# Two transformer blocks on one core: first norm over four tiles, weights' second parts on VectorE, late tiles of the final norm by halves

## The chip, the core and the metric

The kernel runs on one core of a Trainium2 chip. The metric is the time of one execution on the device, in microseconds (us). TensorE multiplies, VectorE (DVE), ScalarE (ACT) and GpSimd (POOL) work element by element, and SyncE (SP) issues most transfers; ACT and POOL issue some. Each engine works off its own queue in order.

## The reference

Two blocks follow one another on x, 1024 tokens of 1024 channels in f32. The parts that the change touches:

```
y = rmsnorm(h, norm_mix_g) @ w_in            # first block: 1024 x 2560
q, k, v = ...; a, g = the last 2 x 512 columns of y
att  = dilated_sliding_attention(q, k, v)    # after a partial rotary of q and k
conv = silu(layernorm(depthwise_conv31(a * sigmoid(g))))
h = h + concat(att, conv) @ w_out
... cross attention, MLP, the whole second block ...
out = rmsnorm(h, lnf_g_2)                    # the final norm
```

## The kernel before

**Precision.** Every f32 operand of a product is cut into a rounded first part (hi, ScalarE, line 128 or 131) and a second part, the rest (lo = src - hi, lines 129 and 132); three matmuls give one product. Weights are split in halves of 512 rows by `w_s` (line 139): a 512 KB load into one of two `raw` buffers, hi on ScalarE, lo on `b.wlo`. A `raw` buffer takes the next load when both parts have been read. The parts lie in 12 `w` tiles, four to a set of weights, which are used in turn.

**Start** (`mix_part`). Eight tiles of 128 tokens are loaded, with the first weights between them. `norm_T` takes them in pairs: sum of squares on ScalarE (line 267), a chain of small VectorE instructions for the inverse root (`rsqrt`, line 244), a scaling (line 293), then 16 TensorE transposes (line 240) whose 128x256 results are split into `xT` (lines 131, 132). `xT[0]` holds tokens 0 to 511, `xT[1]` the rest; a product with `xT[0]` needs tiles 0 to 3.

**First projections.** For each half of the a and g columns, `gemm_s` (line 206) makes g and a for two groups of 128 channels, first over `xT[0]`, then over `xT[1]`: 16 products of 24 matmuls. ScalarE takes tanh of g (line 443), VectorE forms u (line 448). Then v: 16 tiles of 24 matmuls (lines 177 to 179), each copied out of PSUM by ScalarE (line 470) into one of four `t2k` buffers and stored by SP (line 471). Then q and k: four sets of weights, eight half passes of four tiles each, with the rotary on VectorE (line 493) and a transposed, split copy to memory (`stage`).

**Convolution.** Its 120 taps (line 422, one VectorE instruction each, 128 x about 1016) lie in a background list; `pump(us)` takes from the list at set points, at a booked cost of 1.1 for a tap.

**Order.** The instructions of each engine are put in a fixed order when the program is built, by a scheduler with its own model of durations: of what its model calls ready it takes what was written earliest; `high_priority(offset=400)` counts as written 400 instructions earlier, and `issue_after(ins)` keeps what follows behind `ins` on the same engine.

**End.** In the last MLP product `ff_down` makes the last three of the 112 steps tile by tile, so the sums for half 0 of tiles 4, 5, 6 and 7 come one after another. `final_norm` (line 1222) goes through the tiles in order: `finish` adds the late sum (line 1068), ScalarE squares both halves (line 1231), VectorE finds the inverse root for the one tile, scales both halves with the gain (line 1240), and SP and ScalarE store them (line 1243). The next tile's add is issued behind the scaling of the tile before.

Of the kernel before, what the change touches and what calls it, by code (L numbers as in the profile page):

```python
# [12 lines left out]
BF16 = mybir.dt.bfloat16  # L13
AF = mybir.ActivationFunctionType
ALU = mybir.AluOpType
# [4 lines left out]
P = 128  # L20
S = 1024
D = 1024
KT = D // P
NT = S // P
EPS = 1e-6
# [4 lines left out]
def fp(ap):  # L30
    return ap.bitcast(F32)


class Builder:
# [90 lines left out]
    def split(self, hi, lo, src, scale=None, eng=None):  # L125
        nc = self.nc
        if scale is None:
            nc.scalar.activation(hi, src, AF.Copy)  # L128
            (eng or nc.vector).tensor_tensor(out=lo, in0=src, in1=fp(hi), op=ALU.subtract)  # L129
        else:  # L130
            nc.scalar.activation(hi, src, AF.Copy, scale=scale)
            nc.vector.scalar_tensor_tensor(
                out=lo, in0=src, scalar=scale, in1=fp(hi), op0=ALU.mult, op1=ALU.subtract
            )

    def wtile(self, shape, dt=F32R, name="w"):
        return self.wpool.tile(list(shape), dt, tag="w", name=self.nm(name))

    def w_s(self, *parts):


        tiles = []
        for hf in range(2):
            raw = self.rpool.tile([P, 4, 256], F32, tag="raw", name=self.nm("raw"))
            c = 0
            for w in parts:
                n = w.shape[1]
                self.wq.dma_start(
                    out=raw[:, :, c : c + n],
                    in_=w[hf * 512 : (hf + 1) * 512, :].rearrange("(k p) n -> p k n", p=P),  # L150
                )
                c += n
            hi, lo = self.wtile([P, 4, 256]), self.wtile([P, 4, 256])
            self.split(hi, lo, raw, eng=self.wlo)
            tiles.append((hi, lo))

        def get(k, c0, c1):
            hi, lo = tiles[k // 4]
            return hi[:, k % 4, c0:c1], lo[:, k % 4, c0:c1]

        return get

    def w_t(self, w):

# [191 lines left out]
def mem_norm(b):  # L356
    nc = b.nc
    raw = []
    for t in range(2):
        r = b.slot(29 + t, name="mem")  # L360
        nc.sync.dma_start(out=r, in_=b.i["mem"][0, t * P : (t + 1) * P, :])
        raw.append(r)
    tl = [b.slot(20 + n, (P, 4, 256), F32R, "memT") for n in range(4)]
    memT = [(tl[k // 4][:, k % 4, :], tl[2 + k // 4][:, k % 4, :]) for k in range(KT)]
    b.norm_T(raw, b.g_mem, [memT], 2)
    return memT
# [22 lines left out]
def mix_part(b):  # L389
    nc, i = b.nc, b.i  # L390
    w_in = i["w_in"][0]
    b.xk_d = b.dram.tile([4, P, 2, 2, 256], F32, name="xk_d")
    b.xv_d = b.dram.tile([4, P, 2, 2, 256], F32, name="xv_d")
    b.wlo = nc.gpsimd
    xc = i["x"][0].rearrange("(l c) d -> c l d", c=4)
    raw = [b.slot(16 + t, name="x") for t in range(NT)]
    load = lambda t: nc.sync.dma_start(out=raw[t], in_=xc[t // 2, (t % 2) * P : (t % 2 + 1) * P, :])
    (g_mix,) = b.columns("g_mix", [i["norm_mix_g"].rearrange("a (k p) -> (a k) p", p=P)], nc.scalar)
    for t in range(4):
        load(t)  # L400
    wg0 = b.w_s(w_in[:, 2048:2304])
    for t in range(4, NT):
        load(t)
    wa0 = b.w_s(w_in[:, 1536:1792])
    xT = b.halves(range(0, 8), range(8, 16))
    b.norm_T(raw, g_mix, xT, 2)
    b.consts()


# [22 lines left out]
    for half in range(2):  # L432
        wg = b.w_s(w_in[:, 2304:2560]) if half else wg0
        wa = b.w_s(w_in[:, 1792:2048]) if half else wa0
        for js in ((0,), (1,)):
            for mm in range(2):
                m = 2 * half + mm
                if js == (0,):
                    th[m] = b.slot(24 + mm, name="th")
                    u[m] = b.slot(26 + m, name="u")  # L440

                def ev_g(j, ps, m=m):
                    nc.scalar.activation(th[m][:, j * 512 : j * 512 + 512], ps, AF.Tanh, scale=0.5)

                def ev_a(j, ps, m=m):
                    o = u[m].rearrange("p (l c) -> p c l", c=4)[:, 2 * j : 2 * j + 2, :]
                    v3 = lambda a: a.rearrange("p (c l) -> p c l", c=2)
                    nc.vector.scalar_tensor_tensor(
                        out=o, in0=v3(th[m][:, j * 512 : j * 512 + 512]), scalar=1.0, in1=v3(ps),
                        op0=ALU.add, op1=ALU.mult,  # L450
                    )

                b.gemm_s(wg, mm * P, xT, ev_g, js)
                b.gemm_s(wa, mm * P, xT, ev_a, js)
                if js == (1,):
                    conv_ops(m)
                    if m:
                        b.pump(7)
        if half == 0:
            memT = mem_norm(b)  # L460

# [2 lines left out]
    for n in range(2):  # L464
        w = b.w_s(w_in[:, 1024 + n * 256 : 1024 + n * 256 + 256])
        for t in range(NT):
            ps = b.mm()
            b.mm3(ps[:, :256], [(x, w(k, 0, 256)) for k, x in enumerate(b.tok(xT, t))])
            st = b.t2k((P, 256))
            nc.scalar.copy(out=st, in_=ps[:, :256])  # L470
            nc.sync.dma_start(out=b.v_d[t * P : (t + 1) * P, n * 256 : n * 256 + 256], in_=st)
            b.pump(3.5)


# [3 lines left out]
    for p in range(4):  # L478
        w = b.w_s(w_in[:, p * P : p * P + P], w_in[:, 512 + p * P : 512 + p * P + P])
        for half in range(2):  # L480
            y = b.slot((24, 25, 30)[(2 * p + half) % 3], (P, 4, 256), name="y")
            for t4 in range(4):
                ps = b.mm()
# [9 lines left out]
            tt = lambda o, a, c, op: nc.vector.tensor_tensor(out=o, in0=a, in1=c, op=op)  # L493
# [58 lines left out]
    last = []  # L552
# [21 lines left out]
    h = [b.slot(16 + t, name="h") for t in range(NT)]  # L574
# [636 lines left out]
def finish(b, t, after):  # L1211

    if t in b.late:
        with b.tc.high_priority(offset=400), b.tc.issue_after(after.ins):
            b.late.pop(t)()
# [5 lines left out]

def final_norm(b, h, g, out):

    nc = b.nc
    last = None
    for t in range(NT):
        finish(b, t, last)
        sq = b.small(2, "fsq")
        for n in range(2):
            junk = b.slot(8 + (2 * t + n) % 8, (P, 512), BF16, "junk")  # L1230
            nc.scalar.activation(junk, h[t][:, n * 512 : n * 512 + 512], AF.Square, accum_out=sq[:, n : n + 1])
        ms = b.small(1, "fms")
        nc.vector.tensor_scalar(
            out=ms, in0=sq[:, 0:1], scalar1=sq[:, 1:2], scalar2=1.0 / D, op0=ALU.add, op1=ALU.mult
        )
        nc.vector.tensor_scalar(out=ms, in0=ms, scalar1=EPS, scalar2=None, op0=ALU.add)
        r = b.rsqrt(ms)
        for n in range(2):
            sl = slice(n * 512, n * 512 + 512)
            last = nc.vector.scalar_tensor_tensor(  # L1240
                out=h[t][:, sl], in0=h[t][:, sl], scalar=r, in1=g[:, sl], op0=ALU.mult, op1=ALU.mult
            )
            (nc.sync, nc.scalar)[n].dma_start(out=out[0, t * P : (t + 1) * P, sl], in_=h[t][:, sl])


def bias_tables(b):
# [91 lines left out]
class Front:  # L1338
# [18 lines left out]
    def load(self, h):  # L1357
        b, nc = self.b, self.nc
        b.x1_d = b.dram.tile([S, D], F32, name="x1_d")
        self.gf = b.slot(24, name="gf")  # L1360
        nc.gpsimd.dma_start(out=self.gf, in_=b.i["norm_final_g"].partition_broadcast(P))
        self.xT = b.halves(range(8, 16))
        self.w, self.raw = [], []
        for q in range(2):
            self.raw.append(b.kpool.tile([P, 4, 256], F32, tag=f"k{q}", name=b.nm("raw")))
            nc.gpsimd.dma_start(
                out=self.raw[q],
                in_=b.i["w_in_2"][0, q * 512 : (q + 1) * 512, 2560:2816].rearrange("(k p) n -> p k n", p=P),
            )
# [21 lines left out]
    def roots(self):  # L1391
        b, nc = self.b, self.nc
        tt = lambda o, a, q, op: nc.vector.tensor_tensor(out=o, in0=a, in1=q, op=op)
        v0, v1, rr = self.v[:, 0:4], self.v[:, 4:8], self.rr[:, 0:4]
        nc.vector.tensor_scalar(out=v0, in0=v0, scalar1=1.0 / D, scalar2=EPS, op0=ALU.mult, op1=ALU.add)
        r1 = self.r1 = b.rsqrt(v0, 4)
        tt(rr, r1, r1, ALU.mult)
        tt(rr, rr, v1, ALU.mult)
        nc.vector.tensor_scalar(out=v1, in0=rr, scalar1=1.0 / D, scalar2=EPS, op0=ALU.mult, op1=ALU.add)
        tt(rr, b.rsqrt(v1, 4), r1, ALU.mult)  # L1400

    def scaled(self, h, t, at):

        b, nc, q = self.b, self.nc, t % 4
        x1 = b.slot(at, name="x1")
        nc.scalar.activation(x1, h[t], AF.Copy, scale=self.r1[:, q : q + 1])
        nc.gpsimd.dma_start(out=b.x1_d[t * P : (t + 1) * P, :], in_=x1)
        nc.vector.tensor_scalar(out=h[t], in0=h[t], scalar1=self.rr[:, q : q + 1], scalar2=None, op0=ALU.mult)
# [501 lines left out]
```

## Time and profile before

| what | value |
| --- | --- |
| time, median of 3 | 3015.11 us (3013.32 to 3016.35) |
| time of the profiled execution | 3015.72 us |
| its span, first to last instruction | 3013.9 us, mean granted TensorE clock 0.984 |
| PE busy | 2895.5 us, 96% of the span |
| DVE, ACT, POOL busy | 72%, 41%, 13% |

A row of the profile names the engine, the line of the kernel, the operation, what it writes and reads, and how often. The busy share is an average over stages with different limits; the rows further down are taken by stage.

### The profile page before, as it was taken

How to read it: one execution, taken by the hardware profiler on the slowest of the kernel's cores; microseconds unless marked ns; L12 is line 12 of the kernel's file. 1: busy time of each engine (PE TensorE's matmuls, PEld its weight loads, DVE VectorE, ACT ScalarE, POOL GpSimd, SP SyncE). 2: the span in 40 equal slices, each digit the busy share in tenths (PEclk: the TensorE clock that was granted, in tenths of full speed). 3: DMA queues.
4: the chain of work that ended last, by engine and by line, in shares of the span. 5: the costliest groups of instructions: out<-in, count | busy, mean ns of one | idle time of the engine just before them, and what ended most of it. 6: DMA issues, size and time to landing. Idle time of an engine off the chain costs nothing.

```text
span 3013.9 us, 40030 instructions
## 1 busy us (share of the span) xinstructions
PE 2895.5 (96%) x14596; PEld 2438.7 (81%) x14596; DVE 2162.4 (72%) x3889; ACT 1227.5 (41%) x2256; POOL 379.2 (13%) x411
## 2 busy tenths in 40 slices
PE   7899899999999999999999999999999999999997
PEld 5798788788887788888787788898788878888886
DVE  6997787565487776997658777554344776669976
ACT  4122566242253222444655655454211532224444
POOL 2440110000012331000021222200000011100000
PEclk9999899999999999999999999999999999999999
DMA  3135664311124767653231333567842233366522
GB/s 128 49 92 160 178 188 135 99 43 43 50 105 143 230 213 282 246 188 105 72 109 52 101 101 113 174 193 236 281 143 81 98 112 112 109 255 237 182 91 84
DMA packets 251733, 422.86 MB, mean 140 GB/s; under 512 B 27893, under 2 KB 129808, under 8 KB 251536
## 3 DMA queue, kind: packets, MB, share of 16 engines
q1 hardware_dynamic: 213040, 304.29, 31.5%
q0 software_dynamic: 30416, 101.33, 9.7%
q10 hardware_dynamic: 8080, 14.69, 1.3%
q8 instruction: 115, 1.88, 0.3%
q14 instruction: 82, 0.67, 0.1%
HBM read 310.75 MB, written 111.69 MB: 140 GB/s over the span
## 4 chain that ended last, share of the span: by engine, by line
PE 78%; DVE 9%; DMA 5%; ACT 3%; issue 2%; POOL 2%; SPq 1%; DVEq 0%; ACTq 0%; POOLq 0%
PE fd L1182 19%; PE mm L206 18%; PE ff L1009 15%; PE mm L177 5%; PE mm L179 5%; PE mm L178 5%; PE ff L992 2%; PE pv L668 2%; PE tp L734 2%; POOL w L129 1%; PE pv L1708 1%; PE tp L240 1%; DMA bt<-rpb_d 1%; ACT w L128 1%; DVE w L129 1%
## 5 line engine op out<-in xcount | busy, mean ns | idle before, releaser
L1182 PE MATMUL fd<-part,part 128*128 128x512 f32 x2688 | 616.0, 390 | 1.0 <-DVE part L129 1.0
L1182 PEld LDWEIGHTS fd<-part,part 128*128 128x128 f32 x2688 | 504.2, 188 | 110.4 <-DVE part L129 5.8
L1009 PE MATMUL ff<-x,w 128*128 128x512 f32 x2352 | 541.7, 392 | 13.8 <-ACT w L128 7.5
L1009 PEld LDWEIGHTS ff<-x,w 128*128 128x128 f32 x2352 | 443.7, 189 | 111.4 <-ACT w L128 9.2
L206 PE MATMUL mm<-xh,w 128*128 128x512 f32 x1792 | 530.7, 393 | 0.3 <-ACT lruC L1580 0.3
L206 PEld LDWEIGHTS mm<-xh,w 128*128 128x128 f32 x1792 | 336.9, 189 | 68.8 <-ACT lruC L1580 1.4
L128 ACT ACTIVATE part<-keep 128x512 fp32r<-128x512 f32 x384 | 223.8, 623 | 249.5 <-PE fd L1182 243.5
L206 PE MATMUL mm<-xl,w 128*128 128x512 f32 x896 | 316.1, 393 | 0.0
L129 DVE TENSOR_TENSOR part<-keep,part 128x512 fp32r<-128x512 f32 x384 | 250.0, 687 | 44.6 <-ACT part L128 43.9
L128 ACT ACTIVATE w<-raw 128x1024 fp32r<-128x1024 f32 (+1 forms) x132 | 134.9, 1033 | 273.5 <-PE mm L178 111.7
L129 POOL TENSOR_TENSOR w<-raw,w 128x1024 fp32r<-128x1024 f32 x54 | 172.7, 3202 | 444.7 <-ACT w L128 422.5
L206 PEld LDWEIGHTS mm<-xl,w 128*128 128x128 f32 x896 | 168.9, 189 | 33.8 <-issue 0.4
L232 DVE TENSOR_TENSOR h<-h,mm 128x512 f32<-128x512 f32 x176 | 119.8, 686 | 78.6 <-PE mm L179 78.0
L422 DVE SCALAR_TENSOR_TENSOR acc<-u,conv_wh,acc 128x1023 f32<-128x1023 f32 (+14 forms) x120 | 171.7, 1471 | 3.1 <-ACT acc L417 1.3
L177 PE MATMUL mm<-w,xh 128*128 128x256 f32 x512 | 147.9, 289 | 13.5 <-ACT t2k L470 10.3
L852 DVE TENSOR_TENSOR t2k<-ff,t2k 128x512 f32<-128x512 f32 x140 | 96.4, 688 | 82.5 <-PE ff L1009 81.1
L178 PE MATMUL mm<-w,xh 128*128 128x256 f32 x512 | 146.7, 287 | 0.0
L179 PE MATMUL mm<-w,xl 128*128 128x256 f32 x512 | 146.6, 286 | 0.0
L128 ACT ACTIVATE w<-wr 128x512 fp32r<-128x512 f32 x156 | 94.3, 630 | 119.2 <-PE ff L1009 55.5
L974 POOL DMA_DIRECT2D hid_d<-t2k x128 | 70.0, 547 | 489.2 <-DVE t2k L852 265.1
L129 DVE TENSOR_TENSOR w<-raw,w 128x1024 fp32r<-128x1024 f32 (+1 forms) x78 | 91.6, 1180 | 50.2 <-ACT w L128 50.1
L129 DVE TENSOR_TENSOR w<-wr,w 128x512 fp32r<-128x512 f32 x156 | 104.5, 687 | 15.4 <-ACT w L128 14.0
(362 smaller groups left out, 5160.0 us busy)
## 6 DMA issues: line engine op xcount, KB each, us to landing
hid_d<-t2k POOLq DMA_DIRECT2D x128, 256.0 KB, 2.9
x<-hid_d SPq DMA_DIRECT2D x128, 256.0 KB, 4.7
keep<-hid_d SPq DMA_DIRECT2D x96, 256.0 KB, 6.0
raw<-in_w_in_dram SPq DMA_DIRECT2D x38, 512.0 KB, 3.8
qk_d<-t2k SPq DMA_DIRECT2D x64, 256.0 KB, 2.5
wr<-in_w_up_dram SPq DMA_DIRECT2D x32, 512.0 KB, 4.0
keep<-in_w_down_dram SPq DMA_DIRECT2D x64, 256.0 KB, 5.3
wr<-in_w_ff_dram SPq DMA_DIRECT2D x32, 512.0 KB, 3.7
```

What stands on the lines that cost most here:

```text
L128: nc.scalar.activation(hi, src, AF.Copy)
L129: (eng or nc.vector).tensor_tensor(out=lo, in0=src, in1=fp(hi), op=ALU.subtract)
L177: nc.tensor.matmul(ps, sh, mh, start=(i == 0), stop=False)
L178: nc.tensor.matmul(ps, sh, ml, start=False, stop=False)
L179: self.last = nc.tensor.matmul(ps, sl, mh, start=False, stop=(i == n - 1))
L206: self.last = nc.tensor.matmul(pj[j], a, b, start=(k == 0 and q == 0), stop=(k == nk - 1 and q == 2))
L232: self.added[t] = self.nc.vector.tensor_tensor(out=hs, in0=hs, in1=ps, op=ALU.add)
L422: nc.vector.scalar_tensor_tensor(out=acc[m][:, lo:hi], in0=u[m][:, lo + d : hi + d], scalar=w(k), in1=acc[m][:, lo:hi], op0=ALU.mult, op1= ...
L852: tt = lambda o, x, y, op: nc.vector.tensor_tensor(out=o, in0=x, in1=y, op=op)
L974: stored.append(nc.gpsimd.dma_start(out=hid[2 * c + f, :, j * 512 : (j + 1) * 512], in_=o))
L1009: b.last = nc.tensor.matmul(ps, l[:, k, :], r, start=(opens and k == 0 and q == 0), stop=(k == 3 and q == 2), skip_group_check=True)
L1182: last = nc.tensor.matmul(ps[q], l[:, sl], r, start=(c == 0 and x == 0), stop=(c == C - 1 and x == 2))
```

## The change

The first norm takes tiles 0 to 3 in one go and tiles 4 to 7 in another, with 128x512 transposes and splits; the second parts of the weights of the first block (20 instructions) go from GpSimd to VectorE; one `pump` is halved; the stores of v go from SP's queue to ScalarE's; the final norm of tiles 4 to 7 is regrouped.

```diff
+    def w_s(self, *parts, later=False):      # later: loads now, splits when the caller says so
...
-    b.wlo = nc.gpsimd
...
-    wg0 = b.w_s(w_in[:, 2048:2304])
+    wg0, splits = b.w_s(w_in[:, 2048:2304], later=True)
     for t in range(4, NT):
         load(t)
-    wa0 = b.w_s(w_in[:, 1536:1792])
     xT = b.halves(range(0, 8), range(8, 16))
-    b.norm_T(raw, g_mix, xT, 2)
+    def normed(xs):
+        r = b.rms(xs)
+        for t, x in enumerate(xs):
+            nc.vector.tensor_scalar(out=x, in0=x, scalar1=r[:, t : t + 1], scalar2=None, op0=ALU.mult)
+    def turned(j, xs, ks=range(KT)):
+        for k in ks:
+            ps = b.sc() if k % 2 else b.tp()
+            b.transposes(ps, [x[:, k * P : (k + 1) * P] for x in xs])
+            last = b.split(*xT[j][k], ps, scale=g_mix[:, k : k + 1])
+        return last
+    with b.tc.high_priority(offset=400):
+        normed(raw[:4])
+        splits(0)
+        turned(0, raw[:4], range(0, 4))
+        splits(1)
+        hi, lo = turned(0, raw[:4], range(4, 8))
+    with b.tc.issue_after(hi.ins), b.tc.issue_after(lo.ins):
+        wa0 = b.w_s(w_in[:, 1536:1792])
+        normed(raw[4:])
...
                 b.gemm_s(wg, mm * P, xT, ev_g, js)
+                if m == 1 and js == (0,):
+                    with b.tc.high_priority(offset=400), b.tc.issue_after(b.last.ins):
+                        turned(1, raw[4:])
...
-                        b.pump(7)
+                        b.pump(3.5 if m == 2 else 7)
...
-            nc.sync.dma_start(out=b.v_d[...], in_=st)
+            nc.scalar.dma_start(out=b.v_d[...], in_=st)
...
 def final_norm(b, h, g, out):     # tiles 0 to 3 as before, then:
+    for t in range(4, NT):
+        nc.scalar.activation(junk(t, 1), half(t, 1), AF.Square, accum_out=ms[:, t : t + 1])
+        last = tt(half(t, 1), half(t, 1), g[:, 512:1024], ALU.mult)
+    last = nc.vector.tensor_scalar(
+        out=ms[:, 4:8], in0=ms[:, 4:8], scalar1=1.0 / D, scalar2=EPS, op0=ALU.mult, op1=ALU.add)
+    def whole(t):                  # late add of half 0, and its square
+        finish(b, t, last)
+        nc.scalar.activation(junk(t, 0), half(t, 0), AF.Square, accum_out=sq[:, t : t + 1])
+        last = b.added[t]
+    def gained(t):                 # half 0 times the gain
+        left[t] = b.slot(23 + t, (P, 512), name="hg")
+        last = tt(left[t], half(t, 0), g[:, 0:512], ALU.mult)
+    def roots(t):                  # inverse roots of tiles t and t + 1 together
+        with b.tc.issue_after(last.ins):
+            v = ms[:, t : t + 2]
+            nc.vector.scalar_tensor_tensor(out=v, in0=sq[:, t : t + 2], scalar=1.0 / D, in1=v, op0=ALU.mult, op1=ALU.add)
+            return b.rsqrt(v, 2)
+    def scaled(t, n, r, act):      # times the inverse root (ScalarE if act), and the store
...
+    for t in (4, 5):
+        whole(t)
+        gained(t)
+    whole(6)
+    r = roots(4)
+    whole(7)
+    for t in (4, 5):
+        scaled(t, 0, r, False)
+    for t in (4, 5):
+        scaled(t, 1, r, True)
+    for t in (6, 7):
+        gained(t)
+    r = roots(6)
+    for t in (6, 7):
+        scaled(t, 0, r, False)
+        scaled(t, 1, r, True)
```

## Rows read from the trace of the kernel before

**Rows 1.** TensorE waits, 126 to 300 us: wait, releaser, us in all, times, longest.
```profile
PE mm L177 <- ACT t2k L470: 10.3, 2, 6.3
PE mm L177 <- DVE u L448: 3.1, 1, 3.1
```
**Rows 2.** Stages: us; busy PE, PEld, DVE, ACT, POOL (instructions); PE clock, DMA share, GB/s.
```profile
22.40:56.00 33.60, 27.77 (x134) 21.69 (x133) 29.15 (x74) 19.41 (x41) 9.87 (x4) 0.95 0.28 94
56.00:126.30 70.30, 70.30 (x313) 58.20 (x312) 54.91 (x42) 10.41 (x14) 11.86 (x4) 1.00 0.10 31
126.30:186.00 59.70, 46.62 (x361) 46.01 (x359) 59.63 (x42) 12.67 (x21) 43.17 (x6) 0.91 0.20 61
186.00:289.40 103.40, 102.96 (x848) 102.54 (x848) 82.99 (x102) 24.18 (x54) 12.68 (x6) 0.98 0.42 130
```
**Rows 3.** ScalarE's timeline, 126 to 187 us: start, us, instruction, idle before and releaser.
```profile
143.16 1.06 ACT L128 ACTIVATE w<-raw 128x1024 fp32r<-128x1024 f32 x1 [13.02 <-DMA raw<-in_w_in_dram]
...
185.90 0.37 ACT L470 COPY t2k<-mm 128x256 f32<-128x256 f32 x1 [14.72 <-DMA v_d<-t2k]
```
**Rows 4.** GpSimd's timeline, 74 to 232 us.
```profile
128.79 13.86 POOL L129 TENSOR_TENSOR w<-raw,w 128x1024 fp32r<-128x1024 f32 x2 [39.34 <-ACT w L128]
...
161.75 23.74 POOL L129 TENSOR_TENSOR w<-raw,w 128x1024 fp32r<-128x1024 f32 x2 [11.33 <-ACT w L128]
...
217.50 2.42 POOL L129 TENSOR_TENSOR w<-raw,w 128x1024 fp32r<-128x1024 f32 x1
```
**Rows 5.** VectorE's timeline of the same stretch.
```profile
74.54 17.30 DVE L422 SCALAR_TENSOR_TENSOR acc<-u,conv_wh,acc 128x1009 f32<-128x1009 f32 x7 [1.31 <-ACT acc L417]
...
104.32 10.79 DVE L422 SCALAR_TENSOR_TENSOR acc<-u,conv_wh,acc 128x1021 f32<-128x1021 f32 x9
...
137.91 68.49 DVE L422 SCALAR_TENSOR_TENSOR acc<-u,conv_wh,acc 128x1012 f32<-128x1012 f32 x43
```
**Rows 6.** The chain that ended last, 0 to 160 us: start, us, what.
```profile
17.08 2.16 DVE sm L249
...
21.00 0.21 PE sc L240
...
31.60 0.11 PE sc L240
...
56.16 62.14 PE mm L206 x274
...
152.25 0.12 PE mm L179
```
**Rows 7.** Timeline of all engines, 0 to 95 us.
```profile
7.43 0.17 DVE L268 TENSOR_SCALAR sm<-sm 128x2 f32<-128x2 f32 x1 [7.43 <-ACT t2k L267]
...
9.80 1.42 DVE L293 TENSOR_SCALAR x<-x,sm 128x1024 f32<-128x1024 f32 x2
9.92 1.06 ACT L267 ACTIVATE t2k<-x 128x1024 bf16<-128x1024 f32 x1 [0.35 <-DMA x<-in_x_dram]
...
22.42 1.22 PE L206 MATMUL mm<-xh,w 128*128 128x512 f32 x2
```
**Rows 8.** VectorE groups, 300 to 330 us, where it makes second parts: busy us, mean ns.
```profile
L129 DVE TENSOR_TENSOR w<-raw,w 128x1024 fp32r<-128x1024 f32 x2 | 2.4, 1224 | 0.0
```
**Rows 9.** VectorE groups by shape, 92 to 104 us.
```profile
L422 DVE SCALAR_TENSOR_TENSOR acc<-u,conv_wh,acc 128x1020 f32<-128x1020 f32 x1 | 1.3, 1275 | 0.0
...
L422 DVE SCALAR_TENSOR_TENSOR acc<-u,conv_wh,acc 128x1012 f32<-128x1012 f32 x1 | 1.3, 1267 | 0.0
```
**Rows 10.** VectorE's timeline, 2990.7 us to the end of the span.
```profile
2990.79 0.69 DVE L1068 TENSOR_TENSOR h<-h,fd 128x512 f32<-128x512 f32 x1 [8.18 <-PE fd L1182]
...
3009.31 1.42 DVE L1240 SCALAR_TENSOR_TENSOR h<-h,sm,gl 128x512 f32<-128x512 f32 x2
```
**Rows 11.** One VectorE scaling of 128x512 by line: ns min/median/max.
```profile
L1520 DVE TENSOR_SCALAR t2k<-t2k x16: 414/420/2614, 1510.1 to 1795.8; 128x512 f32<-128x512 f32 x16
```
**Rows 12.** SP's issues of the stores of v by line: ns min/median/max.
```profile
L471 SPq DMA_DIRECT2D v_d<-t2k x16: 320/430/607, 151.4 to 198.6; - x16
```

More of the change, by code (lines that the diff above doesn't have):

```diff
@@ L127, in split, with splits @@
         if scale is None:
-            nc.scalar.activation(hi, src, AF.Copy)
-            (eng or nc.vector).tensor_tensor(out=lo, in0=src, in1=fp(hi), op=ALU.subtract)
-        else:
-            nc.scalar.activation(hi, src, AF.Copy, scale=scale)
-            nc.vector.scalar_tensor_tensor(
+            first = nc.scalar.activation(hi, src, AF.Copy)
+            second = (eng or nc.vector).tensor_tensor(out=lo, in0=src, in1=fp(hi), op=ALU.subtract)
+        else:
+            first = nc.scalar.activation(hi, src, AF.Copy, scale=scale)
+            second = nc.vector.scalar_tensor_tensor(
                 out=lo, in0=src, scalar=scale, in1=fp(hi), op0=ALU.mult, op1=ALU.subtract
             )
+        return first, second
     def wtile(self, shape, dt=F32R, name="w"):
         return self.wpool.tile(list(shape), dt, tag="w", name=self.nm(name))
-    def w_s(self, *parts):
-        tiles = []
+    def w_s(self, *parts, later=False):
+        tiles, raws = [], []
+        def splits(hf):
+            hi, lo = self.wtile([P, 4, 256]), self.wtile([P, 4, 256])
+            self.split(hi, lo, raws[hf], eng=self.wlo)
+            tiles.append((hi, lo))
         for hf in range(2):
@@ L152, in w_s @@
                 c += n
-            hi, lo = self.wtile([P, 4, 256]), self.wtile([P, 4, 256])
-            self.split(hi, lo, raw, eng=self.wlo)
-            tiles.append((hi, lo))
+            raws.append(raw)
+            if not later:
+                splits(hf)
         def get(k, c0, c1):
@@ L159, in get @@
             return hi[:, k % 4, c0:c1], lo[:, k % 4, c0:c1]
-        return get
+        return (get, splits) if later else get
     def w_t(self, w):
@@ L470, in mix_part @@
             nc.scalar.copy(out=st, in_=ps[:, :256])
-            nc.sync.dma_start(out=b.v_d[t * P : (t + 1) * P, n * 256 : n * 256 + 256], in_=st)
+            nc.scalar.dma_start(out=b.v_d[t * P : (t + 1) * P, n * 256 : n * 256 + 256], in_=st)
             b.pump(3.5)
@@ L1224, in final_norm, with store @@
     nc = b.nc
-    last = None
-    for t in range(NT):
-        finish(b, t, last)
+    tt = lambda o, x, y, op: nc.vector.tensor_tensor(out=o, in0=x, in1=y, op=op)
+    half = lambda t, n: h[t][:, n * 512 : n * 512 + 512]
+    left = {}
+    junk = lambda t, n: b.slot(8 + (2 * t + n) % 8, (P, 512), BF16, "junk")
+    def store(t, n, src=None):
+        src = half(t, n) if src is None else src
+        (nc.sync, nc.scalar)[n].dma_start(out=out[0, t * P : (t + 1) * P, n * 512 : n * 512 + 512], in_=src)
+    for t in range(4):
         sq = b.small(2, "fsq")
         for n in range(2):
-            junk = b.slot(8 + (2 * t + n) % 8, (P, 512), BF16, "junk")
-            nc.scalar.activation(junk, h[t][:, n * 512 : n * 512 + 512], AF.Square, accum_out=sq[:, n : n + 1])
+            nc.scalar.activation(junk(t, n), half(t, n), AF.Square, accum_out=sq[:, n : n + 1])
         ms = b.small(1, "fms")
@@ L1238, in final_norm @@
         for n in range(2):
-            sl = slice(n * 512, n * 512 + 512)
-            last = nc.vector.scalar_tensor_tensor(
-                out=h[t][:, sl], in0=h[t][:, sl], scalar=r, in1=g[:, sl], op0=ALU.mult, op1=ALU.mult
-            )
-            (nc.sync, nc.scalar)[n].dma_start(out=out[0, t * P : (t + 1) * P, sl], in_=h[t][:, sl])
+            nc.vector.scalar_tensor_tensor(
+                out=half(t, n), in0=half(t, n), scalar=r, in1=g[:, n * 512 : n * 512 + 512], op0=ALU.mult, op1=ALU.mult
+            )
+            store(t, n)
+    sq, ms = (b.small(8, n) for n in ("fl", "fm"))
+    for t in range(4, NT):
+        nc.scalar.activation(junk(t, 1), half(t, 1), AF.Square, accum_out=ms[:, t : t + 1])
+        last = tt(half(t, 1), half(t, 1), g[:, 512:1024], ALU.mult)
+    last = nc.vector.tensor_scalar(
+        out=ms[:, 4:8], in0=ms[:, 4:8], scalar1=1.0 / D, scalar2=EPS, op0=ALU.mult, op1=ALU.add
+    )
+    def whole(t):
+        nonlocal last
+        finish(b, t, last)
+        nc.scalar.activation(junk(t, 0), half(t, 0), AF.Square, accum_out=sq[:, t : t + 1])
+        last = b.added[t]
+    def gained(t):
+        nonlocal last
+        left[t] = b.slot(23 + t, (P, 512), name="hg")
+        last = tt(left[t], half(t, 0), g[:, 0:512], ALU.mult)
+    def roots(t):
+        nonlocal last
+        with b.tc.issue_after(last.ins):
[3 more added lines that the diff above has]
+    def scaled(t, n, r, act):
+        x = half(t, 1) if n else left[t]
+        c = r[:, t % 2 : t % 2 + 1]
+        if act:
+            nc.scalar.activation(x, x, AF.Copy, scale=c)
+        else:
+            nc.vector.tensor_scalar(out=x, in0=x, scalar1=c, scalar2=None, op0=ALU.mult)
+        store(t, n, x)
+    for t in (4, 5):
[14 more added lines that the diff above has]
+        scaled(t, 1, r, True)
 def bias_tables(b):
```

## Prediction

> **What bounds the kernel now.** I read the page first: TensorE is busy for 2895.5 of 3013.9 us, so time can be won only where it waits or works at half speed. The next views were its waits, then the stages, then the timelines of what it waits for.
>
> Two stretches matter. In the first 289 us, TensorE works without a gap only from 56 to 126 us; from 22.4 to 56 us it lacks 5.8 us, and from 126.3 to 186 us it lacks 13.1 us and runs at a mean clock of 0.91 [rows 2]. The waits of the second stretch are 10.3 us for ScalarE's copy of v (two waits, the longer 6.3) and 3.1 us for u on VectorE [rows 1]. Neither is slow itself. The copy stands behind a split of weights that had waited 13.02 us for its load, and later the copy waits 14.72 us for a store of v [rows 3]. The load waits for a `raw` buffer, and the store stands on SP's queue behind such a load. What holds the buffer is the second part on GpSimd: two of them take 13.86 and 23.74 us, where one alone takes 2.42 [rows 4]. VectorE suffers as well: beside GpSimd 7 taps take 17.30 us and 43 take 68.49, while 9 taps with GpSimd idle take 10.79 [rows 5], which is 2.5, 1.6 and 1.2 us for one. In the start the chain shows the same: a step of 0.16 us of the small chain takes 2.16 [rows 6], and three like it follow before 43 us.
>
> The other stretch is the end. The four late sums come 9 matmuls of 0.227 us [rows 6], 2.0 us, apart, the first just before 2990.79, so TensorE is done at 2996.9; but the four tiles follow each other on VectorE at 5 us each, from the add at 2990.79 to the last scaling, which ends at 3010.7 [rows 10].
>
> **Start, part by part.** The fourth tile's square begins at 9.92 and takes 1.06 us; from the first step of the small chain at 7.43 to the scaling at 9.80 are 2.37 us, and two scalings take 1.42 [rows 7]. For four tiles at once: 11.1 + 2.4 + 4 x 0.7 = 16.3 us. From there TensorE always has something. Its work up to the last of the 384 matmuls of the first projections is 384 x 0.227 = 87.1 us (62.14 us for 274) plus 80 transposes, 64 of x and 16 of mem, at 0.11 = 8.8 us [rows 6]. I add 3 us because it begins at the lower of its two clock levels (1.2 GHz; a transpose takes 0.21 at 21.00 and 0.11 at 31.60 [rows 6]). That ends at 115 us instead of 126.3. The first product could also be held up by its operands: eight splits of 0.7 us and a second part of 1.2 on VectorE, some 7 us from 17 us on, beside TensorE's own 11 us at low clock; so they are covered. The second set of weights loads as soon as `raw` is free, near 17 and 21 us, and is due at 33, after two products; behind its loads on SP stand only those of mem and the next weights, due after 58. Bounds: 7 us, if 4 us of gaps stay, and 11. I take **10**.
>
> **v, q and k.** Their work is 1152 matmuls at 0.12 us, the step of rows 6, and 56 transposes at 0.11: 144.4 us. They take 163.1 (126.3 to 289.4 [rows 2]), so 18.7 are lost: 13.4 in waits [rows 1], the rest in the low clock after each. The change removes the slow second parts. One costs 1.22 us on VectorE [rows 8], and 16 of the 20 fall after 56 us. That is 20 us more for VectorE, against 43 taps x (1.59 - 1.20) = 17 us and 7 x 1.3 = 9 us that its taps give back [rows 5]: about even. In the q and k stage, where VectorE had 20 us free of 103 [rows 2], 8 of them take 10. The 16 stores of v leave SP's queue for ScalarE's, at 0.43 us an issue [rows 12] 7 us in all, where 47 of 60 are free [rows 2]. Copies and hi splits stand behind each there, and it waits only for the copy just before it, not for SP's loads. The halved `pump` shifts three or four taps later, into VectorE's free time. From 18.7 I leave 3.7 for order and lag, since VectorE is still full until about 180 us. Bounds: 4 and 18.7. I take **15**.
>
> A rule of the Trainium skill (GPSIMD Engine Reference, section 4.1, Engine selection) says that GpSimd is about twice as slow as VectorE at an operation on two inputs. Alone on GpSimd the second part takes 2.42 us against 1.22, which agrees; beside taps it takes 7 to 12, which the rule doesn't have. By the rule alone the swap would free a buffer 1.2 us sooner, three times over, and this term would be about 4 instead of 15.
>
> **End.** After the add for tile 6, which ends at 2995.5, VectorE has: the roots of 4 and 5, the pair chain of 2.4 us [rows 7]; the add for tile 7, 0.6; two scalings at 0.36 (0.42 busy [rows 11], less the overlap); two products with the gain at 0.6; the roots of 6 and 7, 2.4; together 7.9, to 3003.4. Then each engine scales two halves; ScalarE's two, at 0.6 with a store between them, end near 3005. Before, it was 3010.7. The squares and gain products of the second halves (four of 0.6 us on each engine) move ahead of 2990, where VectorE idles for 8.18 us [rows 10]. The same last store follows in both. Bounds: 4.5, if the add for tile 7 is put ahead of the first roots and they wait for it, and 6.8. I take **6**.
>
> Nothing else changes, and what stands behind an earlier stage moves with it.
>
> **Rivals.**
> 1. *Second parts stand behind the taps.* On VectorE the second parts for q and k are written after 79 of the taps. If the order keeps them behind, TensorE waits: first taps near 61 us, 79 x 1.19 = 94, five u of 0.95, eight second parts of 1.15: 169, but TensorE is due at 115 + 46 = 161. Eight us and 2 of low clock make the gain 21, and the time 2994. Against it: taps of two channel groups stand mixed at 92 to 104 us (1020 long from the first, 1012 from the second [rows 9]), though all of the first were written earlier, so what is written later does slip in. Chance 0.18. The Trainium skill (TensorE: Matmul & The Clock Gate, section Architectural detail: the array is 16x 32x32, not 1x 128x128) says that VectorE's queue is strictly first in, first out. By that rule nothing can mend such an order while it runs; no row here shows an exception.
> 2. *The waits for late loads stay.* hi stands on ScalarE in front of the copies in a fixed order; if the loads still land later than that order supposes, the 10.3 us stay and the term of 15 becomes 5: gain 21, 2994. For it: the order comes from a model of durations that missed before. Against: what was late was GpSimd. Chance 0.12.
> 3. *The taps stay slow*, because something else than GpSimd slows them. At 1.59 a tap, 79 take 126 us, the second parts for q and k are done at 201, and q and k end at 299, 10 later than before; one more late load of 6 us, less the 6 of the end: 3025, slower. It is slower from about 1.6 us a tap on. Against: 1.20 whenever GpSimd idles [rows 5]. Chance 0.05.
>
> **The numbers.** Gain 10 + 15 + 6 = 31 on the profiled execution of 3015.7 us, whose span is 3013.9 with 1.8 around it; it lies 0.6 above the median of 3015.1. So 2984 for the median. The forecast has 0.65 (2979 to 2997 by its bounds: 11 + 18.7 + 6.8 = 36.5 and 7 + 4 + 4.5 = 15.5, the last giving 2999.6 if all are bad together). Its own bounds and rivals 1 and 2 lie within 2975 to 3002, where the lower end leaves 4 us for orders further on that fall out better. That range leaves out rival 3. A difference of 0.2%, 6 us, is about what a measurement of this kernel can tell from no change: faster by that 0.90, within it 0.05 (the terms near nothing together; I take it from the 0.95 of the forecast and rivals 1 and 2), slower 0.05 (rival 3).
>
> **What would show it.** Start: four scalings in a row near 13.5 to 16.3 us, the first matmul of the first projections before 20 instead of 22.42, the last near 115. Middle: GpSimd without work on weights up to 290 us, taps at 1.2 us throughout, second parts at 1.22 between them, no wait of TensorE over 3 us between 126 and 260, and q and k finished near 264 instead of 289.4. End: two pair chains after 2 x 2 late sums, the last scaling about 8 us after the last matmul instead of 14. I am wrong if TensorE waits for a second part w on VectorE at the change from v to q and k, if taps stay above 1.4 us, or if the stages after 290 us come out longer than before.

## The result, and the profile after

The changed kernel takes 2984.51 us (median of 3, 2983.72 to 2988.67) against 3015.11; the ratio is 0.9892, 95% interval 0.9878 to 0.9906. The profiled execution's span falls from 3013.9 to 2981.9 us. Three executions in the runs further down that were far slower than all others of their kernel (3592.73, 4793.56 and 8262.68 us) are left out of every median and ratio.

The stages of the profile after, as in [rows 2]; each line gives the stretch and its length in us; busy PE, PEld, DVE, ACT, POOL (instructions); PE clock, DMA share, GB/s.

```profile
16.30:56.00 39.70, 38.81 (x202) 32.01 (x201) 31.18 (x72) 24.94 (x43) 0.00 (x0) 1.00 0.35 116
56.00:115.30 59.30, 59.30 (x263) 49.13 (x262) 52.69 (x46) 12.12 (x14) 0.00 (x0) 1.00 0.12 36
115.30:180.00 64.70, 64.70 (x540) 64.66 (x540) 63.52 (x56) 16.10 (x30) 0.00 (x0) 1.00 0.33 98
180.00:259.80 79.80, 79.79 (x671) 79.55 (x669) 64.09 (x91) 18.54 (x41) 1.53 (x2) 1.00 0.43 134
```

The first projections end at 115.35 us instead of 126.28, and v, q and k at 259.8 instead of 289.4. In the v, q and k stage TensorE lacks 0.01 of 144.5 us and the clock stays at its upper level, 2.4 GHz. From 16 us to 259.8 us GpSimd computes nothing; the 1.53 us are DMA issues.

Some of TensorE's waits from 115 us on, as in [rows 1]. All of these lie behind q and k, in the attention; the waits for copies of v and for u are gone.

```profile
PE tp L247 <- DVE y L522: 5.3, 1, 5.3
PE tp L247 <- DVE z L562: 3.8, 1, 3.8
...
PE tp L247 <- DVE sm L266: 2.4, 1, 2.4
```

VectorE's timeline, which answers to [rows 5, 7 and 8]: the chain for four tiles, their scalings, and later second parts of 1.21 between taps. Twenty taps take 23.78 us, 1.19 each.

```profile
10.99 0.17 DVE L275 TENSOR_SCALAR sm<-sm 128x4 f32<-128x4 f32 x1 [7.85 <-ACT t2k L274]
...
12.87 1.23 DVE L129 TENSOR_TENSOR w<-raw,w 128x1024 fp32r<-128x1024 f32 x1
...
14.39 2.74 DVE L415 TENSOR_SCALAR x<-x,sm 128x1024 f32<-128x1024 f32 x4
...
131.10 1.22 DVE L129 TENSOR_TENSOR w<-raw,w 128x1024 fp32r<-128x1024 f32 x1
...
134.56 23.78 DVE L448 SCALAR_TENSOR_TENSOR acc<-u,conv_wh,acc 128x1018 f32<-128x1018 f32 x20
158.27 1.21 DVE L129 TENSOR_TENSOR w<-raw,w 128x1024 fp32r<-128x1024 f32 x1
...
264.88 2.57 DVE L448 SCALAR_TENSOR_TENSOR acc<-u,conv_wh,acc 128x1011 f32<-128x1011 f32 x2
...
267.97 1.58 DVE L448 SCALAR_TENSOR_TENSOR acc<-u,conv_wh,acc 128x1009 f32<-128x1009 f32 x1
```

The last two of these rows are three taps that now stand inside the attention, between its transposes; before, the last taps stood at 281.57 to 288.07, before q and k ended at 289.4.

ScalarE's timeline, as in [rows 3]: the splits still wait for loads, for 3.49 and 5.11 us instead of 13.02, but no wait of TensorE follows.

```profile
136.69 1.06 ACT L128 ACTIVATE w<-raw 128x1024 fp32r<-128x1024 f32 x1 [3.49 <-DMA raw<-in_w_in_dram]
...
164.23 1.06 ACT L128 ACTIVATE w<-raw 128x1024 fp32r<-128x1024 f32 x1 [5.11 <-DMA raw<-in_w_in_dram]
```

In the kernel before, what the loads stood behind shows in the waits of SP's queue, 110 to 290 us: 86.7 us for second parts on GpSimd, which read the `raw` buffers.

```profile
SPq L148 <- POOL w L129: 86.7, 8, 49.4
```

The end, which answers to [rows 10]: VectorE's late sums and scalings, then ScalarE's timeline and the DMA issues from 2960 us on.

```profile
2964.39 0.69 DVE L1097 TENSOR_TENSOR h<-h,fd 128x512 f32<-128x512 f32 x1 [7.77 <-PE fd L1211]
...
2970.67 0.68 DVE L1097 TENSOR_TENSOR h<-h,fd 128x512 f32<-128x512 f32 x1
...
2975.22 0.88 DVE L1312 TENSOR_SCALAR hg<-hg,sm 128x512 f32<-128x512 f32 x2
```

```profile
2975.22 1.33 ACT L1310 ACTIVATE h<-h,sm 128x512 f32<-128x512 f32 x2 [0.83 <-DVE sm L266]
2975.97 0.95 ACTq L1262 DMA_DIRECT2D out_dram<-h  x2
```

```profile
out_dram<-hg SPq DMA_DIRECT2D x4, 256.0 KB, 3.0
out_dram<-h ACTq DMA_DIRECT2D x4, 256.0 KB, 3.2
```

TensorE ends at 2970.47 us, the last scaling at 2976.55, the span at 2981.9: 11.4 us from TensorE's end to the end of the span, where it was 17.0 (2996.87 to 3013.9).

### The profile page after: what moved, and what is told of

It reads as the page before. It is cut to its first block, busy times and chain, and to the rows that moved or that the text cites. A ratio compares the mean times of both kernels' runs of the same rounds, so it can differ in the third digit from the quotient of the medians.

```text
span 2981.9 us, 39926 instructions
## 1 busy us (share of the span) xinstructions
PE 2885.4 (97%) x14596; PEld 2430.9 (82%) x14596; DVE 2138.4 (72%) x3854; ACT 1228.3 (41%) x2244; POOL 297.8 (10%) x391
## 4 chain that ended last, share of the span: by engine, by line
PE 80%; DVE 10%; DMA 4%; ACT 3%; issue 2%; POOL 0%; SPq 0%; ACTq 0%; DVEq 0%; POOLq 0%
PE fd L1211 19%; PE mm L213 17%; PE ff L1038 16%; PE mm L184 5%; PE mm L185 5%; PE mm L186 5%; PE ff L1021 2%; PE pv L697 2%; PE tp L763 2%; PE pv L1795 1%; PE tp L247 1%; DVE lruE L1526 1%; DMA bt<-rpb_d 1%; DVE w L129 1%; DVE lruC L1525 1%
## 5 line engine op out<-in xcount | busy, mean ns | idle before, releaser
L129 DVE TENSOR_TENSOR w<-raw,w 128x1024 fp32r<-128x1024 f32 (+1 forms) x98 | 116.0, 1188 | 51.2 <-ACT w L128 51.0
L448 DVE SCALAR_TENSOR_TENSOR acc<-u,conv_wh,acc 128x1016 f32<-128x1016 f32 (+14 forms) x120 | 147.9, 1276 | 2.3 <-ACT acc L443 1.3
L184 PE MATMUL mm<-w,xh 128*128 128x256 f32 x512 | 145.3, 284 | 0.0
L129 POOL TENSOR_TENSOR w<-raw,w 128x1024 fp32r<-128x1024 f32 x34 | 91.4, 2689 | 318.5 <-ACT w L128 276.7
```

Of the source, the lines that this page charges most:

```text
L129: second = (eng or nc.vector).tensor_tensor(out=lo, in0=src, in1=fp(hi), op=ALU.subtract)
L184: nc.tensor.matmul(ps, sh, mh, start=(i == 0), stop=False)
L448: nc.vector.scalar_tensor_tensor(out=acc[m][:, lo:hi], in0=u[m][:, lo + d : hi + d], scalar=w(k), in1=acc[m][:, lo:hi], op0=ALU.mult, op1= ...
```

## The experiments

Spans are compared with 3013.9 (before) and 2981.9 (changed). Three executions of the changed kernel had spans of 2981.9, 2986.9 and 2982.7 us; those of the kernel before, timed again beside each group of runs, went from 3010.4 to 3023.5. So a difference of 3 us in one span says little by itself; a stage compared by its own rows says more. Times are medians, and each ratio is taken against the kernel before as timed beside that run (medians from 3015.11 to 3019.30 us); ratios can be compared with each other and with the 0.9892 of the changed kernel, times only roughly.

**One part alone, and one part undone**

```diff
 # e1_before_dve: the kernel before
-    b.wlo = nc.gpsimd
```

> The kernel before with one edit: the second parts of the first block's weights on VectorE instead of GpSimd. My reading (GpSimd and the taps slow each other): taps at 1.2 us throughout, v, q and k in about 145 to 150 us instead of 163.1, and the start shorter by most of its four held-up steps of 2 us; in all 18 to 26 us faster, 2989 to 2997. If the second parts stand behind the taps (first rival): not more than 8 us faster. If GpSimd is only twice as slow and nothing else (the page's rule): about 4 us faster, 3011.

2991.99 us, ratio 0.9911 (0.9895 to 0.9928), span 2989.8. The first projections end at 118.6 us, 7.7 earlier, and v, q and k take 145.3 us (118.6 to 263.9) instead of 163.1: its two stages, clock at 1.00 in both.

```profile
118.60:156.00 37.40, 37.40 (x313) 37.38 (x312) 37.40 (x33) 7.50 (x15) 0.00 (x0) 1.00 0.22 71
156.00:263.90 107.90, 107.21 (x898) 106.82 (x897) 93.86 (x117) 26.86 (x56) 1.52 (x2) 1.00 0.44 134
```

One removed line brings 24 of the 32 us of span, and by the ratios 0.89 of 1.08 per cent.

```diff
 # e2_after_pool: the changed kernel
+    b.wlo = nc.gpsimd
```

> The changed kernel with the second parts of the first block's weights put back on GpSimd. My reading: taps at 1.5 us and more beside GpSimd, waits of TensorE behind late weights come back in part (the stores of v no longer stand on SP's queue): 12 to 22 us slower than the changed kernel, 2997 to 3007. If the gain came from the start by four tiles and the end alone: within 4 us of the changed kernel.

3008.06 us, ratio 0.9962 (0.9947 to 0.9976), span 3006.3, 24 longer than the changed kernel and a little more than the 12 to 22 expected. The first projections end at 123.67 us and v, q and k take 159.1. The copies of v no longer hold TensorE, but VectorE does; its timeline, GpSimd's, and the wait of TensorE:

```profile
123.72 19.23 DVE L449 SCALAR_TENSOR_TENSOR acc<-u,conv_wh,acc 128x1017 f32<-128x1017 f32 x9
```

```profile
160.97 19.50 POOL L129 TENSOR_TENSOR w<-raw,w 128x1024 fp32r<-128x1024 f32 x1 [20.29 <-ACT w L128]
```

```profile
PE mm L184 <- DVE u L475: 11.5, 1, 11.5
```

Nine taps take 19.23 us: in the rows of single taps, four beside a second part take 3.4 each and the other five 1.3. The u behind them comes 11.5 us late. So the wait moved to another engine; its cause, GpSimd's second parts, stayed.

```diff
 # e3_before_end: the kernel before, with final_norm of the changed kernel
```

> The kernel before with the new final norm alone. From the two traces: span after TensorE's end 17.0 us before and 11.4 after, so 5 to 6 us faster, 3009 to 3010. If the earlier store tail was what counted: under 3 us faster.

3013.79 us, ratio 0.9983 (0.9974 to 0.9992), which is 2 to 8 us faster, span 3009.3. TensorE ends at 2998.15, 1.3 us later than before, and the end takes 11.2 us from there instead of 17.0: the part's own gain is 5.8 us.

```diff
 # e4_after_pairs: the changed kernel, with the start of the kernel before
-        normed(raw[:4])
...
+    b.norm_T(raw, g_mix, xT, 2)
```

> The changed kernel with the start by pairs of tiles as before (second parts still on VectorE, stores of v on ScalarE, new end). The start gained 10.8 us in the trace; if half of that came from GpSimd no longer holding up VectorE's small steps, this is 3 to 7 us slower than the changed kernel, 2988 to 2992; if all of it came from the four tiles at once, 11 us slower, 2995; if none, equal.

2988.41 us, ratio 0.9897 (0.9882 to 0.9913), span 2986.3. The first projections end at 118.21 instead of 115.35: the norm over four tiles is worth 2.9 us there. v, q and k take 144.4, as in the changed kernel.

```diff
 # e5_after_vsp: the changed kernel
-            nc.scalar.dma_start(out=b.v_d[t * P : (t + 1) * P, ...], in_=st)
+            nc.sync.dma_start(out=b.v_d[t * P : (t + 1) * P, ...], in_=st)
```

> The changed kernel with the stores of v back on SP's queue. With second parts on VectorE the raw buffers come free in time, so SP's loads should no longer hold the stores long: my reading 0 to 4 us slower than the changed kernel. If SP's queue was what held the copies of v: waits of TensorE of 4 us and more come back, 6 to 10 us slower.

2982.57 us, ratio 0.9882 (0.9866 to 0.9898), span 2982.7, q and k done at 260.4: no difference. With loads on time it does not matter which queue stores v; whether it would with late loads was not run.

```diff
 # e6_after_pump: the changed kernel
-                        b.pump(3.5 if m == 2 else 7)
+                        b.pump(7)
```

> The changed kernel, but after the third channel group 7 taps are let out again instead of 3.5. In the changed kernel the last three taps stand at 264.88 to 269.55 us, behind the last rotary products, in the stretch from the transposes of y (265.11) to those of z (282.67), which takes 17.56 us there and 16.09 in the kernel before, where the taps were done earlier. Theory (the halved number sends the last taps into the start of the attention, where VectorE sets the pace): the stretch takes 16.0 to 16.4 us, and the span becomes 1 to 2 us shorter than the changed kernel's 2981.9. Rival A (the stretch is longer for the order that the other parts bring): it stays at 17 to 18 us and the span within 0.7. Rival B (the halving was needed while the first groups are worked on): TensorE gets a wait of over 2 us before 260 us and the span grows.

2983.04 us, ratio 0.9886 (0.9872 to 0.9901), span 2977.9. TensorE's timeline at the ends of the stretch:

```profile
264.19 1.50 PE L247 MATMUL tp<-ident,y 128*128 128x128 f32 x8 [4.39 <-DVE y L522]
...
280.04 3.14 PE L247 MATMUL tp<-ident,z 128*128 128x128 f32 x12 [3.75 <-DVE z L562]
```

15.85 us, even a little under the 16.0 of the theory, against 17.56 (265.11 to 282.67) in the changed kernel. The span is 4.0 shorter, twice what the stretch gives, and the times are within each other's scatter; rival B's wait does not come, the longest before 260 us is 0.9.

**The rivals' prices**

```diff
 # e7_after_behind: the changed kernel; the first weights of q and k, with their splits
-            nc.vector.scalar_tensor_tensor(
+            b.tapped = nc.vector.scalar_tensor_tensor(
...
-        w = b.w_s(w_in[:, p * P : p * P + P], w_in[:, 512 + p * P : 512 + p * P + P])
+        with b.tc.issue_after(b.tapped.ins) if p == 0 else ExitStack():
+            w = b.w_s(w_in[:, p * P : p * P + P], w_in[:, 512 + p * P : 512 + p * P + P])
```

(`b.tapped` is the tap written last before it.)

> The changed kernel with the first rival made true by order alone: the second parts of the first weights for q and k are queued on VectorE behind every tap written before them. In the changed kernel they run at 158 to 162 us, some 9 taps early. Expected: TensorE waits 8 us at the change from v to q and k and then works some time at its lower clock: 8 to 12 us slower than the changed kernel, 2993 to 2997. If the lag is made up later: within 3 us.

2996.71 us, ratio 0.9937 (0.9924 to 0.9950), span 2994.6, 12.7 longer, just over the 8 to 12 expected. VectorE's timeline, and the TensorE matmul that waits:

```profile
134.29 39.60 DVE L448 SCALAR_TENSOR_TENSOR acc<-u,conv_wh,acc 128x1018 f32<-128x1018 f32 x32
173.81 2.36 DVE L129 TENSOR_TENSOR w<-raw,w 128x1024 fp32r<-128x1024 f32 x2
```

```profile
175.08 0.58 PE L185 MATMUL mm<-w,xh 128*128 128x256 f32 x1 [12.90 <-DVE w L129]
```

The stage takes 159.9 us instead of 144.5: 12.9 of wait and 2.5 more at the lower clock level that follows it (mean granted clock 0.77 from 175 to 185 us, 1.00 behind that). Rival 1 had the mechanism right and its price too low (8 + 2). In the changed kernel the order of the program puts the second parts between taps, at 158.27 instead of 173.81.

```diff
 # e9_after_adds: the changed kernel; results unused
+    spare = b.slot(30, name="spare")
+    for _ in range(6):
+        nc.gpsimd.tensor_tensor(out=spare, in0=u[3], in1=u[2], op=ALU.add)
```

> The changed kernel with six useless GpSimd additions of two 128x1024 operands beside the taps, from about 118 us on; no weights pass through GpSimd. If GpSimd slows the taps by itself: each addition takes 6 to 14 us, the taps beside them 1.6 us and more, VectorE falls 15 to 20 us behind and TensorE waits 5 to 16 us for second parts: slower by as much. If only the late raw buffers counted: taps at 1.2 us and no difference.

2995.65 us, ratio 0.9930 (0.9918 to 0.9942), span 2997.4. VectorE's timeline, then the row of one tap alone, GpSimd's additions (ns min/median/max), and TensorE's wait:

```profile
118.78 26.01 DVE L448 SCALAR_TENSOR_TENSOR acc<-u,conv_wh,acc 128x1015 f32<-128x1015 f32 x11
144.72 1.21 DVE L129 TENSOR_TENSOR w<-raw,w 128x1024 fp32r<-128x1024 f32 x1
```

```profile
119.95 3.42 DVE L448 SCALAR_TENSOR_TENSOR acc<-u,conv_wh,acc 128x1023 f32<-128x1023 f32 x1
```

```profile
L494 POOL TENSOR_TENSOR spare<-u,u x6: 3249/3256/3262, 119.0 to 135.7; 128x1024 f32<-128x1024 f32 x6
```

```profile
PE mm L185 <- DVE w L129: 8.9, 3, 6.6
```

Eleven taps at 1.19 would be 13.1 us; 12.9 more for six additions is 2.15 for each. The single rows show where it goes: six taps take 3.41 to 3.42 us, one per addition, and the others 1.25 to 1.27 (a tap starts some 0.08 before the one ahead of it ends, which makes 1.19 each). The additions take 3.25 us, not the 6 to 14 expected. With nothing but GpSimd's work added, the second part behind the taps is late and TensorE waits.

```diff
 # e12_after_fills: the changed kernel; results unused
+    spare = b.slot(30, name="spare")
+    nc.gpsimd.tensor_tensor(out=spare, in0=u[3], in1=u[2], op=ALU.add)
+    for _ in range(16):
+        nc.gpsimd.memset(spare, 0.0)
```

> The changed kernel with useless work for GpSimd in the same place as the six additions of the other run, but one addition of u[3] and u[2] and behind it sixteen fills of the same spare tile with a constant: GpSimd writes 128x1024 as before, but reads nothing. Beside the six additions 11 taps took 26.0 us, each addition 3.26, which is one tap of 1.19 and 2.07 in which VectorE stands still. Theory (an instruction of GpSimd that reads on-chip memory shuts out a VectorE instruction with two inputs there, one at a time; one that only writes does not): the addition costs about 2.1 us, the taps beside the fills take 1.19 to 1.2, the same 11 taps end near 15.5 us after they begin, q and k end within 3 us of the changed kernel's 259.8, and the span is 1 to 4 us longer. Rival (any work of GpSimd on 128x1024 slows the taps): 11 taps take over 20 us and the span is 8 to 15 us longer.

2984.12 us, ratio 0.9884 (0.9867 to 0.9900), span 2983.2. VectorE's timeline, then GpSimd's instructions on the spare tile:

```profile
117.15 15.31 DVE L448 SCALAR_TENSOR_TENSOR acc<-u,conv_wh,acc 128x1015 f32<-128x1015 f32 x11
132.38 1.21 DVE L129 TENSOR_TENSOR w<-raw,w 128x1024 fp32r<-128x1024 f32 x1
```

```profile
L495 POOL MEMSET spare<- x16: 953/956/957, 120.7 to 136.0; 128x1024 f32 x16
L493 POOL TENSOR_TENSOR spare<-u,u x1: 3254/3254/3254, 117.4 to 117.4; 128x1024 f32<-128x1024 f32 x1
```

One addition costs the eleven taps 2.2 us (15.31 - 13.1), sixteen fills cost them nothing. So it is not GpSimd's being busy or its writing that slows a tap. What the addition does and the fill does not is to read, so the reading is the likely cause; a GpSimd instruction that reads one operand was not run.

**What is left**

```diff
 # e8_after_block2: the changed kernel, second block
-    b.wlo = nc.gpsimd
```

> The changed kernel with the second parts of the second block's weights on VectorE too (34 instructions, 91 us on GpSimd). TensorE loses only about 10 us there in waits, and VectorE is 72% busy; if the same mutual slowing is at work, 3 to 8 us faster than the changed kernel; if TensorE is not held up by it there, within 3 us; if VectorE gets too full beside the recurrences, slower.

2974.26 us, ratio 0.9853 (0.9838 to 0.9868), span 2972.9: 9.0 shorter, a little more than the 3 to 8 expected, and the lowest time of all. The second block's stage, first in the changed kernel, then here:

```profile
1440.00:1960.00 520.00, 505.71 (x2478) 424.85 (x2477) 371.67 (x443) 302.30 (x406) 107.75 (x60) 0.99 0.35 108
```

```profile
1440.00:1951.00 511.00, 504.48 (x2513) 426.44 (x2512) 377.09 (x489) 307.35 (x417) 16.26 (x26) 1.00 0.35 111
```

GpSimd gives up 91 us of work, and VectorE, which takes it over, is busy for 5.4 us more in the same stage, not for 34 x 1.15 = 39.

```diff
 # e10_end_early: the changed kernel; sums and scalings reordered
-    whole(6)
     r = roots(4)
-    whole(7)
+    whole(6)
     for t in (4, 5):
-        scaled(t, 0, r, False)
+        last = scaled(t, 0, r, False)
+        scaled(t, 1, r, True)
...
+    with b.tc.issue_after(last.ins):
+        whole(7)
+        gained(6)
+        gained(7)
```

> The changed kernel, but in the final norm of the late tiles the small chain and the scalings of tiles 4 and 5 come directly behind the second sum, and the last sum, the gain products of 6 and 7 and the second chain come behind these scalings. Theory (after the change the end is set by the four last stores, which go out together with the four before them: 2.1 MB in the 6 us from 2973.6): the stores of tiles 4 and 5 start near 2971 us from the same start of the stage, 2.5 us earlier, the last scalings stay where they are, and the time from TensorE's end to the end of the span falls from 11.4 to 8.5 to 10 us. Rival (the last chain sets the end, and the last sum now waits for the first scalings): it stays at 11 us or grows by up to 1.

2984.45 us, ratio 0.9891 (0.9874 to 0.9907), span 2985.0. From TensorE's end (2973.72) to the end it is 11.3 us, so the rival holds. ScalarE's timeline:

```profile
2974.74 0.95 ACTq L1262 DMA_DIRECT2D out_dram<-h  x2
...
2979.69 0.95 ACTq L1262 DMA_DIRECT2D out_dram<-h  x2
```

The first stores are out 5 us ahead of the last, yet the last two tiles still need 4.7 us from their last scaling (which ends at 2980.27), and that scaling comes 0.5 us later after TensorE's end than in the changed kernel.

```diff
 # e11_all: e6, e8 and e10 together
```

> The changed kernel with three edits together: the second block's second parts on VectorE too (alone 9 us shorter in the span), 7 taps let out again after the third channel group (1 to 2 expected alone), and the last stores apart (1.5 to 3 expected alone). Theory (three stretches that do not touch): the span is near 2969, 2967 to 2971, 11 to 15 us under that of the changed kernel. Rival (orders further on take back what an earlier stretch gains, as 2 to 3 us were taken back behind the first block's attention): 2971 to 2974.

2974.70 us, ratio 0.9859 (0.9844 to 0.9874), span 2973.1: not different from e8_after_block2 alone. The rival's numbers hold; why the 1.7 us of e6_after_pump do not show in the total was not found, and they are no larger than what executions of one kernel differ by.

## Why the prediction was right, point by point

**Start, 10 us.** Measured 10.9 (126.28 to 115.35), inside the bounds of 7 to 11. The first matmul came at 18.81, before the 20 that was asked for. The scalings came 0.9 us later than forecast, at 14.39 to 17.13, because a second part of 1.23 us stood in the small chain. What the text did not separate: the norm over four tiles brings 2.6 to 2.9 us of it (e2_after_pool, e4_after_pairs), GpSimd's leaving 7.7 to 8.3 (e1_before_dve, and the changed kernel against e2_after_pool).

**v, q and k, 15 us.** The mechanism held; this is the mis-sized term, 18.7 measured. The pure work was given as 144.4 us and came out as 144.5; the 3.7 us kept back "for order and lag, since VectorE is still full" were not needed. VectorE is indeed full up to 180 us, but second parts on GpSimd had lengthened twelve of its taps by about 2.0 us each in the kernel before (2.15 for an addition in e9_after_adds), and on VectorE one costs 1.15, so the swap freed VectorE. The text's own rows held that price: it set 20 us of second parts against 26 that the taps give back and called it "about even". It also counted 16 second parts behind 56 us where there are 14 (GpSimd's six in the last of [rows 2] hold two DMA issues), so 17 us stood against 26.

The 7 to 12 us that it read for a second part beside taps are means of unequal pairs. The pair of 23.74 us in [rows 4] is one of 20.46 and one of 3.3, and during the long one the taps run at full pace (VectorE's timeline of the same stretch):

```profile
161.75 20.46 POOL L129 TENSOR_TENSOR w<-raw,w 128x1024 fp32r<-128x1024 f32 x1 [11.33 <-ACT w L128]
```

```profile
160.90 17.86 DVE L422 SCALAR_TENSOR_TENSOR acc<-u,conv_wh,acc 128x1016 f32<-128x1016 f32 x15
```

So slow taps and late buffers are two effects: a second part costs VectorE one lengthened tap, and now and then it waits for many taps, which is what holds a buffer.

By the rule of the factor of two that the prediction weighed (the Trainium skill, GPSIMD Engine Reference, section 4.1) the term would have been 4; e1_before_dve gives 17.8. What that rule lacks stands elsewhere: the Trainium skill, SBUF — State Buffer, section Who interferes with whom, says that a VectorE instruction with two inputs in SBUF, the on-chip memory, contends with a GpSimd instruction that reads SBUF and not with one that only writes. e9_after_adds (2.15 us for an addition) and e12_after_fills (nothing for a fill) agree.

**Two steps without effect or with the wrong sign.** The stores of v on ScalarE's queue, weighed at 7 us of issues beside free time, changed nothing either way (e5_after_vsp). The halved `pump` was said to move three or four taps "into VectorE's free time"; three taps landed in the attention, where VectorE sets the pace, and the stretch from y to z takes 17.56 us, where it takes 16.09 in the kernel before (293.84 to 309.93) and 15.85 in e6_after_pump.

**End, 6 us.** Measured 5.6 in the changed kernel and 5.8 in e3_before_end. The number is luck: two errors of 2 us cancel. The last scaling ends 6.1 us after the last matmul, not 8. The text's terms add up to 7.3 and not to its 7.9, and VectorE works on the second chain (from 2972.14) and the gain products inside the first chain, not behind the first scalings (2973.06). And "the same last store follows in both" is wrong: four stores of 256 KB are issued within 1.2 us and the span ends 5.4 us after the last scaling; before, two were left, 0.7 us apart, and it ended 3.2 us after (3010.73 [rows 10] to 3013.9).

**After 290 us.** "What stands behind an earlier stage moves with it" does not hold exactly: q and k are done 29.6 us earlier, TensorE is done 26.4 earlier. Longer stages after 290 us were one of the text's own signs of being wrong; they came, with 3.2 us of the 29.6. About 1.5 us of these are the taps in the attention. They may be all of it: from the last matmul of q and k to TensorE's end it takes 2708.6 us before, 2711.8 in the changed kernel and 2707.8 in e6_after_pump, one execution each. Differences of that size are no larger than what executions of one kernel differ by, and it was not traced further.

So 10 + 15 + 6 = 31 against 10.9 + 18.7 + 5.6 - 3.2 = 32.0 in the span and 30.6 by the medians. That the total comes so close is in part luck: the v, q and k term was 3.7 too low, and the 3.2 that were lost behind it were not forecast.

**The rivals.** Rival 1 did not occur, but its place and mechanism are real (e7_after_behind). Rival 2 occurred in part: splits still wait for loads, and TensorE does not. Rival 3 did not: taps are at 1.19; that slow taps reach TensorE is shown by e9_after_adds. By the text's own sum (61 + 79 taps + 14 + 98 against 289.4) q and k would end later than before from about 1.47 us a tap on, not 1.6.

## What to carry to other kernels

Work handed to GpSimd is not free for VectorE. Here a 128x1024 instruction of GpSimd that reads two operands lengthened a tap beside it by 2.0 to 2.2 us, more than the 1.15 that VectorE needs for a second part itself, and fills cost nothing; make this comparison before work is handed over. When a wait is traced to an engine that is "not slow itself", follow it back to what holds the buffer, and expect a half-way repair to move the wait to the next engine, as in e2_after_pool. Where every gap went, as in v, q and k, the pure work by rows was a better forecast than pure work plus a reserve.

## What the runs showed of the hardware that was not expected

- GpSimd and VectorE take turns, an instruction at a time: an addition of 128x1024 on GpSimd beside taps takes 3.25 us, one tap of 1.19 and 2.07 for itself, where a second part alone takes 2.42 [rows 4]; each addition lengthens one tap by about 2.15 (e9_after_adds).
- A GpSimd instruction can wait for many taps: in e2_after_pool one second part takes 19.50 us from 160.97 on, while taps follow each other without a gap, 11 of them from 159.16 to 172.28 (13.12 us). The kernel before shows the same (20.46 us from 161.75 on), which is why buffers were late although a second part costs the taps only about 2.1 us. Why it waits there and takes turns in e9_after_adds is not shown.
- Not only instructions with two inputs are held up. In the kernel before, two second parts on GpSimd run from 38.13 to 43.27 us; beside them a scaling with one tensor input takes 2.89 us instead of 0.75, and a step of the small chain 2.34 instead of 0.16. Splits that take one of their inputs from PSUM, TensorE's output memory, keep their 0.48 us beside the second part of 25.61 to 28.01.

```profile
38.15 2.89 DVE L293 TENSOR_SCALAR x<-x,sm 128x1024 f32<-128x1024 f32 x1
40.95 2.34 DVE L248 TENSOR_SCALAR sm<-sm 128x2 int32<-128x2 int32 x1
```

```profile
26.32 0.48 DVE L132 SCALAR_TENSOR_TENSOR xl<-tp,g_mix,xh 128x256 fp32r<-128x256 f32 x1
```

- Sixteen fills of 128x1024 by GpSimd (0.956 us each) cost neighbouring taps nothing (e12_after_fills).
